# Bias table product among the unread transposes of the first norm, with 18 of them in place of 22

## The chip, the cores and the metric

The kernel runs on one core of a Trainium2 chip. What counts is the device time of one execution in microseconds (us): 847.76 us before, the median of 3 runs (847.65 to 847.85).

The core has five engines that run side by side and meet only at semaphores: PE (TensorE: matmuls and transposes; its weight loads are shown apart as PEld), DVE (VectorE), ACT (ScalarE), POOL (GpSimd) and SP (SyncE, which here only issues transfers). Each takes its own instructions in order. Transfers are issued from the queues of SP, ACT and POOL and are moved by 16 DMA engines that all of them share.

## What is computed

One decoder layer on a sequence of 512 tokens with 1024 channels. The first sub-layer normalises x, projects it once, and gives the columns to an attention mixer with 8 heads and to a recurrent mixer with 8 heads; both are projected back, merged by gates and added to x. The second is a gated feed-forward block. Of the reference, this matters here:

```python
h = rmsnorm(x, attn_norm_g[l])
proj = h @ w_in[l]
...
bias = bias_tab[t5_bucket(dist)]          # rel_bias: 32 buckets x 8 heads
sc = jnp.einsum('bqgrd,bkgd->bgrqk', q_b, kw) + bias
```

Each attention score gets a bias that depends on the head and on the bucket of the distance between query and key. The table `rel_bias` has 32 rows and 8 columns.

## The kernel before

**Dense products.** All weights are float32. A weight tile arrives in one of three buffers `raw` (512 KB, issued on SP's queue, line 265). ACT rounds it to a high part `whi` (line 123, the helper of all activations), DVE or POOL subtracts to get the low part `wlo` (line 294), and PE adds three products: high by high, high by low and low by high (line 120, the helper of all matmuls). A `raw` buffer is free for the next load when its low part has been made.

**The first norm.** Four tiles `xt` of 128 tokens are loaded on SP's queue (line 152). On ACT's queue go the identity matrix `ident`, a part of the tile `kc` (line 153), and the gains `pr0` (line 154). Eight small loads `pra` and the rest of `kc` go on POOL's. Three weight tiles are loaded behind `xt`. Then follows a stretch whose order of instructions is written out by hand. PE runs `NWARM` = 22 transposes of the identity into a bank that nobody reads (line 332); the gains' transpose (line 165) was put after 14 of them. ACT squares the four tiles and sums each (with a root for each pair); DVE makes the inverse roots and scales the tiles to `h` (line 130, one half tile on ACT). PE turns `h` by transposes (line 341: 8 for each of the first two tiles, then 8 pairs for the last two). ACT and DVE turn each result into the high part `hh` and the low part `hl`. With these, PE starts its first dense product. Eight PSUM banks are in use: four under the name `ps_mm`, two under `ps_a`, two under `ps_b`; the unread transposes write into one of `ps_b`, and the last two of the eight turned banks are `ps_b` too.

**The bias table.** The bias for each distance is a product: `oh`, a one-hot matrix of 33 rows and 384 distances, by `rbx`, the 32 rows of `rel_bias` and a row of -1e30 for forbidden distances. The result, 8 heads by 384, goes from PSUM to `vb` on ACT. One DMA then writes 16 copies of it into a DRAM tensor `vd`, from which eight transfers on SP's queue (line 902) read the shifted rows 80 us later. In the kernel before, all of this stands between the query projection and the projection of keys and values, in parts of the tile `QK` that the keys fill later. It isn't in an order written by hand; the scheduler put it there:

```python
pt = pa()
mm(pt[0:8, 0:384], rbx, oh, True, True)
act(vb, pt[0:8, 0:384])
```

While this runs, DVE inverts the triangular blocks of the recurrence (62 dependent operations, line 135, and then transposes, lines 728 and 733). PE uses their result in small correction products (`ps_a<-sg,AB`, 32 rows by 32), then starts the compression of keys and values (`ps_mm<-raw,sg`) and the recurrence over 8 chunks, with dense products filling its waits.

## Time and profile before

| What | us |
|---|---|
| median of the runs | 847.76 |
| the profiled execution, its time | 847.76 |
| the profiled execution, its span | 846.0 |
| PE busy | 831.9 |
| DVE busy | 514.7 |
| ACT busy | 405.7 |
| POOL busy | 52.5 |
| first unread transpose on PE | 4.89 |
| first dense matmul on PE | 14.16 |
| bias table product on PE | 152.73 |

A row of the timeline gives the start in us from the span's start, the length in us, the engine (a q behind its name: its queue issued a transfer), the line, the operation, the tile written and the tiles read, their shapes and how many instructions the row joins. Brackets give the engine's idle time just before and what ended it; "issue" stands for none that the profile shows. The ends of matmuls are modelled, and each row has a tail in which the next instruction already runs: the distance of two starts tells what an instruction costs PE. A row that joins several lasts until the end of the last.

### The profile page before, as it was taken

To read this page: it belongs to the slowest core of one execution; us is meant where nothing else is said; L and a number is where in the kernel's file an instruction comes from. 1 tells how busy PE (TensorE), PEld (TensorE's weight loads), DVE (VectorE), ACT (ScalarE), POOL (GpSimd) and SP (SyncE) were. 2 spreads that over 40 slices of the span, in tenths; PEclk is the share of its full clock that TensorE was granted. 3 is DMA by queue.
4 is the path that set the end of the run, shared out by engine and by line. 5 is a ranking of instruction groups with operands and counts; after the bars stand their busy time and mean duration, and the time that the engine had idled before them with its cause. 6 is when DMAs were issued, how large, how long until landed. Compare 5 with 4: busy or idle time off the path is not lost.

```text
span 846.0 us, 12844 instructions
## 1 busy us (share of the span) xinstructions
PE 831.9 (98%) x5097; PEld 676.2 (80%) x5097; DVE 514.7 (61%) x998; ACT 405.7 (48%) x784; POOL 52.5 (6%) x69
## 2 busy tenths in 40 slices
PE   7999999999999999999999999999999999999998
PEld 6777778897777886777788888888888888888886
DVE  5477779963555678888675566666666666322222
ACT  6766645443545677767344454444444444221210
POOL 6200020140000110111000000000000000000000
PEclk9999999999999999999999999999999999999999
DMA  7432222335551320010167023333333332333421
GB/s 231 112 86 62 75 75 76 92 108 151 132 119 50 83 69 13 15 36 26 52 215 221 0 77 98 100 100 100 100 100 95 90 91 98 100 100 112 136 75 50
DMA packets 109104, 78.73 MB, mean 93 GB/s; under 512 B 3869, under 2 KB 97748, under 8 KB 109044
## 3 DMA queue, kind: packets, MB, share of 16 engines
q1 hardware_dynamic: 106512, 73.51, 29.8%
q0 software_dynamic: 1472, 1.86, 1.0%
q10 hardware_dynamic: 1060, 2.55, 1.0%
q8 instruction: 40, 0.66, 0.3%
q14 instruction: 20, 0.16, 0.1%
HBM read 74.56 MB, written 2.29 MB: 91 GB/s over the span
## 4 chain that ended last, share of the span: by engine, by line
PE 52%; DVE 0%; ACT 0%; DVEq 0%; issue 0%
PE ps_mm L120 52%; DVE hl L135 0%; PE ps_a L120 0%; PE ps_b L1181 0%; PE ps_a L200 0%; PE ps_mm L1181 0%; ACT hh L123 0%; PE ps_b L200 0%; DVE x L126 0%; DVEq L1373 0%; PE ps_a L1133 0%
## 5 line engine op out<-in xcount | busy, mean ns | idle before, releaser
L294 DVE TENSOR_TENSOR wlo<-raw,whi 128x1024 fp32r<-128x1024 f32 (+1 forms) x111 | 131.6, 1185 | 189.4 <-PE ps_mm L120 166.8
L120 PE MATMUL ps_mm<-hh,whi 128*128 128x512 f32 (+1 forms) x624 | 243.3, 392 | 0.4 <-ACT hh L123 0.3
L120 PE MATMUL ps_mm<-hl,whi 128*128 128x512 f32 (+1 forms) x624 | 240.9, 388 | 0.3 <-DVE hl L135 0.2
L123 ACT ACTIVATE whi<-raw 128x1024 fp32r<-128x1024 f32 (+3 forms) x124 | 123.4, 996 | 170.3 <-PE ps_mm L120 142.4
L120 PE MATMUL ps_mm<-hh,wlo 128*128 128x512 f32 (+1 forms) x624 | 151.8, 385 | 0.0
L120 PEld LDWEIGHTS ps_mm<-hh,whi 128*128 128x128 f32 x624 | 117.3, 188 | 27.3 <-issue 1.3
L120 PEld LDWEIGHTS ps_mm<-hl,whi 128*128 128x128 f32 x624 | 117.4, 188 | 24.1 <-DVE hl L135 1.0
L120 PEld LDWEIGHTS ps_mm<-hh,wlo 128*128 128x128 f32 x624 | 115.2, 188 | 23.3
L120 PE MATMUL ps_mm<-whi,aT 128*128 128x512 f32 x352 | 84.5, 390 | 0.0
L120 PEld LDWEIGHTS ps_mm<-whi,aT 128*128 128x128 f32 x352 | 65.9, 188 | 14.3 <-issue 0.4
L135 DVE SCALAR_TENSOR_TENSOR cgv<-ps_mm,cw,cgv 128x511 f32<-128x511 f32 (+1 forms) x88 | 65.4, 746 | 1.5
L123 ACT ACTIVATE cgv<-ps_mm,cw 128x512 f32<-128x512 f32 x44 | 34.3, 781 | 22.8 <-PE ps_mm L120 22.8
L120 PE MATMUL ps_mm<-wlo,aT 128*128 128x512 f32 x176 | 44.3, 390 | 0.0
L123 ACT ACTIVATE P<-P,nm 128x512 f32<-128x512 f32 (+3 forms) x64 | 35.4, 554 | 14.9 <-DVE nm L1155 14.9
L123 ACT ACTIVATE aT<-cgv 128x512 fp32r<-128x512 f32 x22 | 13.9, 631 | 56.8 <-DVE cgv L126 56.8
L120 PEld LDWEIGHTS ps_mm<-wlo,aT 128*128 128x128 f32 x176 | 33.1, 188 | 6.9
L123 ACT ACTIVATE cgv<-cgv 128x512 f32<-128x512 f32 x22 | 13.9, 632 | 43.9 <-DVE cgv L135 43.8
L294 POOL TENSOR_TENSOR wlo<-raw,whi 128x512 fp32r<-128x512 f32 (+3 forms) x13 | 20.4, 1573 | 203.6 <-PE ps_mm L120 147.9
L1155 DVE CUSTOM_DVE_ANT_0 P<-ps_a,AB 128x512 f32<-128x512 f32 (+3 forms) x64 | 29.4, 484 | 4.2 <-PE ps_a L120 3.7
L126 DVE TENSOR_TENSOR x<-x,ps_mm 128x512 f32<-128x512 f32 (+1 forms) x17 | 11.1, 656 | 23.9 <-PE ps_mm L120 22.7
L126 DVE TENSOR_TENSOR aT<-cgv,aT 128x512 fp32r<-128x512 f32 x22 | 15.2, 693 | 14.7 <-ACT aT L123 14.7
L120 PE MATMUL ps_a<-KH,qst 128*128 128x512 f32 (+3 forms) x64 | 21.3, 349 | 1.5 <-DVE nm L1155 0.9
(356 smaller groups left out, 1205.5 us busy)
## 6 DMA issues: line engine op xcount, KB each, us to landing
raw<-in_w_up_dram SPq DMA_DIRECT2D x44, 512.0 KB, 3.8
raw<-in_w_in_dram SPq DMA_DIRECT2D x38, 512.0 KB, 3.9
raw<-in_w_down_dram SPq DMA_DIRECT2D x22, 512.0 KB, 3.6
raw<-in_w_out_dram SPq DMA_DIRECT2D x8, 512.0 KB, 3.7
xt<-in_x_dram SPq DMA_DIRECT2D x4, 512.0 KB, 5.7
raw<-in_cmp_w_k_dram SPq DMA_DIRECT2D x4, 512.0 KB, 4.0
raw<-in_cmp_w_v_dram SPq DMA_DIRECT2D x4, 512.0 KB, 4.4
raw<-in_w_proj_b_dram SPq DMA_DIRECT2D x8, 256.0 KB, 2.7
```

Source lines behind the costliest of these rows:

```text
L120: te.matmul(o, lhsT=l, rhs=r, start=start, stop=stop)
L123: sc.activation(o, i, f, **kw)
L126: v.tensor_tensor(o, a, b, op=op)
L135: v.scalar_tensor_tensor(o, a, s, b, op0=op0, op1=op1)
L294: eng.tensor_tensor(lo, raw, hi.bitcast(F32), op=ALU.subtract)
L1155: v.tensor_tensor_reduce(out=P[:, i], in0=sp[:, N * (i - i0):N * (i - i0) + N], in1=BT[:, h, 384 - 128 * qt:512], scale=-1.0, scalar=-NEG, ...
```

## The change

The bias table's product, its eviction and its store move to the first norm. `oh`, `rbx` and `vb` become tiles of their own. Their loads are issued on ACT's queue right behind the identity, ahead of the gains. The row of -1e30 is set by DVE instead of POOL. The product stands on PE behind the sixth unread transpose, into the second `ps_b` bank; `NWARM` falls from 22 to 18. The eviction stands on ACT between the squares of the third and the fourth tile. The store goes on SP's queue, behind the first three weight loads, instead of ACT's.

```diff
-    NWARM = 22
+    NWARM = 18
...
     sc.dma_start(ident, A["consts"][:, 0:128])
+    oh, rbx, vb = (xp.tile([p, n], F32, name=k) for k, p, n in (("oh", 33, 384), ("rbx", 33, 8), ("vb", 8, 384)))
+    v.memset(rbx[32:33], NEG)
+    sc.dma_start(rbx[0:32], A["rel_bias"])
+    sc.dma_start(oh, A["onehot"])
     sc.dma_start(pr0, A["attn_norm_g"][0].rearrange("(r p) -> r p", p=128))
...
+    vd = dp.tile([8, 16 * 385], F32, name="vd")
...
         warm = pb()
+        vps = pb()
         for i in range(NWARM):
             te.transpose(warm[:, 0:128], ident, ident)
+            if i == 5:
+                mm(vps[0:8, 0:384], rbx, oh, True, True)
...
         for t in (2, 3):
             act(hs[t], xt[:, t], AF.Square, accum_out=ssx[:, t:t + 1])
+            if t == 2:
+                act(vb, vps[0:8, 0:384])
+                nc.sync.dma_start(vd.rearrange("h (i m) -> h i m", m=385)[:, :, 0:384],
+                                  vb[:, None, :].to_broadcast([8, 16, 384]))
...
-    oh, rbx, vb = QK[0:33, 2048:2432], QK[0:33, 2440:2448], QK[0:8, 2560:2944]
-    nc.gpsimd.memset(rbx[32:33], NEG)
-    sc.dma_start(rbx[0:32], A["rel_bias"])
-    sc.dma_start(oh, A["onehot"])
-    pt = pa()
-    mm(pt[0:8, 0:384], rbx, oh, True, True)
-    act(vb, pt[0:8, 0:384])
-    vd = dp.tile([8, 16 * 385], F32, name="vd")
-    sc.dma_start(vd.rearrange("h (i m) -> h i m", m=385)[:, :, 0:384], vb[:, None, :].to_broadcast([8, 16, 384]))
```

In the order of instructions that the changed program ends up with, PE runs 6 unread transposes, the product, the gains' transpose and 12 unread transposes. Transfers share eight completion counters in turn, and three more early ones shift the turns: on SP, the first weight load now waits until the identity has landed, the second until the first tile of x, the third until the second. Before, only the third waited, for the identity. The last of the turned banks waits for the eviction, since it reuses the product's bank. On all engines the order of everything else is as before, but for ACT's evictions of keys and values next to the old place, which come tile by tile.

## The prediction

> **What bounds the kernel now.** I read the page's first lines, then the busy time by stretch (start and end, length, then PE, weight loads, DVE, ACT, POOL, the granted clock, the DMA engines' share and GB/s), then the timeline at the two places that the change touches.

> ```profile
> span 846.0 us, 12844 instructions
> PE 831.9 (98%) x5097; PEld 676.2 (80%) x5097; DVE 514.7 (61%) x998; ACT 405.7 (48%) x784; POOL 52.5 (6%) x69
> ...
> 4.88:14.16 9.28, 9.24 (x56) 8.22 (x56) 4.92 (x18) 8.13 (x15) 3.15 (x7) 1.00 1.10 342
> 14.16:150.00 135.84, 135.15 (x721) 104.13 (x722) 103.44 (x173) 84.03 (x176) 17.55 (x22) 1.00 0.31 81
> ...
> 156.00:168.00 12.00, 12.00 (x84) 11.16 (x84) 11.46 (x23) 4.83 (x25) 2.01 (x1) 1.00 0.30 71
> ```

> The profiled execution took 847.76 us, which is the median too: 846.0 of span and 1.76 around it. In 14.16 to 150 PE is busy 135.15 of 135.84, in 156 to 168 all of 12.00, so a microsecond taken from PE's order there, or added ahead of it, moves the end by as much, unless another engine is just behind. The 4.88 to 14.16 stretch is different: PE is as full, but with transposes whose output nobody reads. There the first norm sets the time. The question is what the product saves at 153 us and what it costs before 14 us.

> **What leaves, at 153 us.** The columns are start, length, engine, line, operation.

> ```profile
> 152.41 0.28 PE L120 MATMUL ps_mm<-spare,hl 128*128 128x256 f32 x1
> 152.53 0.28 PE L120 MATMUL ps_mm<-spare,hh 128*128 128x256 f32 x1
> ...
> 152.73 0.81 PE L120 MATMUL ps_a<-QK 33*8 33x384 f32 x2
> 153.06 0.48 PE L120 MATMUL ps_a<-QK 33*8 33x384 f32 x1
> ...
> 153.47 0.39 PE L120 MATMUL ps_mm<-spare,hl 128*128 128x256 f32 x1
> ...
> 153.58 0.48 ACT L123 ACTIVATE QK<-ps_a 8x384 f32<-8x384 f32 x1 [0.96 <-PE ps_a L120]
> ...
> 154.98 0.28 ACT L123 ACTIVATE QK<-ps_mm 128x128 f32<-128x128 f32 x1 [0.92 <-PE ps_mm L120]
> ```

> The projection's matmuls follow each other at 0.12 (152.41 to 152.53). Around the product, two instructions 0.33 apart, they are 0.94 apart (152.53 to 153.47). PE gains 0.94 - 0.12 = 0.82. The eviction (0.48) stands between two idle times of ACT, 0.96 and 0.92: it goes for nothing, as do the issues on ACT's queue and the one-row memset on POOL.

> Does another engine take the 0.82 back? The nearest is DVE, whose inversion and its transposes run unbroken beside PE.

> ```profile
> 163.02 4.51 DVE L728 STREAM_TRANSPOSE sg<-inv 32x1024 f32<-32x1024 f32 x2
> ...
> 168.72 0.10 PEld L120 LDWEIGHTS ps_a<-sg,AB 32*32 32x32 f32 x1 [0.35 <-issue]
> ...
> 180.30 1.29 DVE L126 TENSOR_TENSOR sg<-QK,prm 128x248 f32<-128x248 f32 x2
> ...
> L120 PE MATMUL ps_mm<-raw,sg x64: 378/380/430, 183.0 to 212.3; 128*64 128x256 f32 x64
> ```

> The correction products read sg, ready at 167.53, and start at 168.72: 1.19 of room. The compression's read at 183.0 has 1.4 after 181.59. Both exceed 0.82. Term one: **-0.82**.

> **What arrives, before 14 us.** PE's order becomes 6 transposes, the product, the gains' transpose (L165 now), 12 transposes: 18 for 22. Side by side, the two programs' orders show nothing else moved on PE.

> ```profile
> 4.89 3.25 PE L332 MATMUL ps_b<-kc 128*128 128x128 f32 x14 [4.89 <-DMA kc<-in_consts_dram]
> ...
> 8.07 0.27 PE L165 MATMUL ps_a<-kc,pr 8*128 8x8 f32 x1
> ...
> 8.27 1.97 PE L332 MATMUL ps_b<-kc 128*128 128x128 f32 x8
> ...
> 10.11 0.55 PEld L341 LDWEIGHTS ps_mm<-kc,h 128*128 128x128 f32 x4 [0.28 <-DVE h L130]
> 10.11 0.79 PE L341 MATMUL ps_mm<-kc,h 128*128 128x128 f32 x4
> ...
> 11.18 0.60 PE L341 MATMUL ps_mm<-kc,h 128*128 128x128 f32 x4
> 11.61 0.38 PE L341 MATMUL ps_a<-kc,h 128*128 128x128 f32 x2
> ...
> 12.12 1.13 PE L341 MATMUL ps_mm<-kc,h 128*128 128x128 f32 x8
> 12.63 2.42 ACT L123 ACTIVATE hh<-ps_mm,ang 128x512 fp32r<-128x512 f32 x4 [0.42 <-PE ps_mm L341]
> ...
> 15.47 0.19 PEld L120 LDWEIGHTS ps_mm<-hl,whi 128*128 128x128 f32 x1 [0.32 <-DVE hl L135]
> ```

> Of the unread transposes 14 take 3.25 and 8 take 1.97, so one takes (3.25 - 1.97)/6 = 0.21. Of the turns, of the same shape, four start between 11.18 and 11.61: 0.11 each. The four at 10.11 take 0.79, in between. So PE runs at half rate until about 10.4, though the granted clock stands at 1.00 all along. Four fewer save 0.85. The product's two parts at half rate are 2 x 2 x 0.33 = 1.32, plus 0.15 for the changes of weights (152.53 to 152.73 is 0.20 in place of 0.12, 153.06 to 153.47 is 0.08 over 0.33). The train grows by 1.32 + 0.15 - 0.85 = 0.6. It ended at 10.0 (8.27 + 8 x 0.21) and ends near 10.6, or 10.5, as its last few run at the faster rate. The first turn could start at 10.11, when DVE had its tile; now PE makes it wait. Sixteen turns at 0.11 take 1.8 and end near 12.3, so the pair at 12.12, which releases hh at 12.63, starts 0.2 later. From there the delay goes through hh and hl to PE, which waits for hl at 15.47.

> [...]

> **When the operands land** decides more. PE must have them by 6.2 (4.89 + 6 x 0.21).

> ```profile
> 0.75 0.40 ACTq L153 DMA_DIRECT2D kc<-in_consts_dram  x1
> ...
> 1.26 0.54 ACTq L154 DMA_DIRECT2D pr<-in_attn_norm_g_dram  x1
> ...
> 4.70 1.06 ACT L123 ACTIVATE h<-xt 128x1024 f32<-128x1024 f32 x1 [2.01 <-DMA xt<-in_x_dram]
> ...
> 6.00 1.06 ACT L123 ACTIVATE h<-xt 128x1024 f32<-128x1024 f32 x1 [0.15 <-DMA xt<-in_x_dram]
> ...
> 5.00:6.00 1.00, 1.00 (x5) 1.00 (x6) 0.00 (x0) 0.85 (x2) 0.46 (x1) 1.00 1.03 409
> ...
> pra<-in_rwkv_w_dram POOLq DMA_DIRECT2D x1, 2.0 KB, 5.4
> ...
> QK<-in_onehot_dram ACTq DMA_DIRECT2D x1, 49.5 KB
> ...
> QK<-in_rel_bias_dram ACTq DMA_DIRECT2D x1, 1.0 KB, 1.4
> ```

> The two new loads take pr's place in ACT's queue, at about 1.3 and 1.8; pr goes third. In a quiet stretch such a load lands after 1.4, which gives 3.2. Under the x loads, which fill the engines (409 GB/s), the identity needed 4.1 (0.75 to 4.89) and a 2 KB load on POOL's queue 5.4. So the one-hot table lands between 3.2 and 7.2. I take the identity's 4.1 (5.9) plus 0.3 to 0.7 for third place, 6.2 to 6.6: it is nearest in queue and size. A wait of 0.3 replaces unread transposes that would run at half rate by ones after the rise, and costs 0.1. So the start costs 0.3. The gains' transpose behind the product needs pr, one place later, at about 7.9: 1.3 more than the table.

> **Beside it, at nothing.** ACT's eviction of the product stands between the squares.

> ```profile
> 8.34 0.19 ACT L123 ACTIVATION_READ_ACCUMULATOR h<-xt 128x1 f32 x1
> 8.91 1.06 ACT L123 ACTIVATE h<-xt 128x1024 f32<-128x1024 f32 x1 [0.38 <-DMA xt<-in_x_dram]
> ...
> 10.52 1.06 ACT L123 ACTIVATE whi<-raw 128x1024 fp32r<-128x1024 f32 x1
> 11.48 0.73 ACT L123 ACTIVATE h<-xt,ssx 128x512 f32<-128x512 f32 x1
> ...
> 2.64 2.27 SPq L265 DMA_DIRECT2D raw<-in_w_in_dram  x2
> ...
> 15.59 0.37 SPq L265 DMA_DIRECT2D raw<-in_w_in_dram  x1
> ```

> Its 0.48 fills ACT's 0.38 of waiting for the fourth x tile, so the fourth square is 0.1 late, inside PE's 0.2; without that cover it would be 0.48, and behind it wait the second root, the first weight's rounding at 10.52 and the half tile at 11.48. If the product ended after 8.5, ACT and these would wait with it. On SP, the order of the changed program makes the first weight load wait for the identity (4.89) instead of going at 2.64. The x loads ahead hold the engines to 8.91, so it is still queued 3 us early; were it not, up to 2.25 would fall on 10.52. The 49.5 KB of table at 409 GB/s push everything behind it back 0.12, again beside PE's delay. The table's store, now on SP behind the third weight load, has only the load at 15.59 after it, held by POOL: nothing. The memset goes to DVE, idle then.

> **Sum.** -0.82 + 0.2 + 0.1 = -0.5: 847.76 - 0.5 = **847.2**. Bounds of this case: start cost 0 (clock up early) to 0.6 (operands at 7.0), so 846.9 to 847.5.

> **Rivals.**
> *The table is late.* If each small load lets one quarter of x (1.30, 4.70 to 6.00) go ahead, the identity follows the first, rel_bias the second, the table the third, which lands about 7.3. The product runs 7.5 to 8.9, the gains follow, and twelve transposes end near 11.2 with the rate rising at 10.4; turns end at 13.0, a start cost of 0.9 (ACT's fourth square, 0.5 late behind the eviction, lies beside it). Net +0.1: **847.8**, no gain. For it: POOL's 5.4. Against: the identity's 4.1. [...] No row here settles it, as pr's landing is hidden.

> *The clock rises late* (the slower side). The product uses 33 rows and 8 columns, perhaps after an idle gap; if this doesn't keep the rate's rise at 10.4 and all 16 turns run at 0.21, they end at 10.6 + 3.4 = 14.0 instead of 12.1, start cost 1.9, net +1.1: **848.9**. It decides from an operand landing past about 7, or if so small a product doesn't count. For it: the rate rose at 10.4 after 5.5 us of full-width work without a gap, and no row shows that less would do. Against it: 18 of the 22 transposes stay. [...]

> *The gain is absorbed* at 168.72: if DVE ran 0.7 late against PE there, 0.3 of the 0.82 would go and the sum would be **847.5**. DVE's whole chain starts from PE's own results, so it moves with it.

> **Chances.** Forecast 0.52, table late 0.26, clock late 0.15, absorbed 0.04, other 0.03. The range 846.7 to 848.6 holds the forecast's own 846.9 to 847.5, the late table, the absorbed gain and the lighter part of the clock's case; its ends lie 0.2 past the forecast's lower bound and 0.3 short of that case's price. About 0.2% (1.7 us) is what a measurement of this kernel tells from no change: below 846.1 would need twice the product's price, 0.03; above 849.5 takes the clock's case with a longer wait, 0.08; between, 0.89.

> **What would show it.** After: no product near 153 us and 0.12 between the projection's matmuls; the product on PE at 6.3 to 6.7 without a long wait for its loads; first hh 0.2 to 0.4 after 12.63; the product at 168.72 about half a microsecond earlier. A start of the product past 7, or turns 0.21 apart after 10.6, shows a rival; a first rounding that waits for its weight past 10.7 shows that the load's wait on SP wasn't hidden.

## The result and the profile after

The changed kernel takes 851.64 us, the median of 6 runs (850.79 to 851.98), against 847.86 for the kernel before on the same chip (847.65 to 848.04): a ratio of 1.0044, 95% interval 1.0031 to 1.0056. It is slower by 3.8 us, where the forecast was 0.5 faster; the time lies 3.0 above the top of the range. The profiled execution took 851.36, with a span of 849.6.

Three stretches show where. First the start, PE's timeline (start, length, engine, line, operation):

```profile
5.10 1.54 PE L340 MATMUL ps_b<-kc 128*128 128x128 f32 x6 [5.10 <-DMA kc<-in_consts_dram]
6.62 1.43 PE L120 MATMUL ps_b<-oh,rbx 33*8 33x384 f32 x2
7.98 0.27 PE L169 MATMUL ps_a<-kc,pr 8*128 8x8 f32 x1
8.19 2.82 PE L340 MATMUL ps_b<-kc 128*128 128x128 f32 x12
10.80 1.06 PE L355 MATMUL ps_mm<-kc,h 128*128 128x128 f32 x4
...
12.34 0.60 PE L355 MATMUL ps_mm<-kc,h 128*128 128x128 f32 x4
...
15.16 0.50 PE L120 MATMUL ps_mm<-hh,whi 128*128 128x512 f32 x1
```

The product stands at 6.62, where the forecast had it, and its row shows no wait for the table. But the four turns at 10.80 still take 0.21 each; only those at 12.34 are at 0.11. PE's rate rises at about 12.1 instead of 10.4, and the first dense matmul starts at 15.16 instead of 14.16: +1.0. Of this the longer train is about 0.6, as forecast, and the six turns at half rate about 0.4. Another 0.2 is chance: the identity landed at 5.10 instead of 4.89, and three kernels without the early table had it at 4.99 to 5.20. Small waits of PE that fell away give back 0.2.

The product is gone at 153, and the gain is there: PE reaches the correction products at 168.78 instead of 168.72, so 0.94 of the 1.0 is back. There it is lost again. DVE and POOL of the kernel before, then of the changed one:

```profile
162.57 0.19 DVE L135 SCALAR_TENSOR_TENSOR Tm<-inv 128x31 f32<-128x31 f32 x1
162.79 0.19 DVE L135 SCALAR_TENSOR_TENSOR inv<-Tm,inv 128x31 f32<-128x31 f32 x1
...
163.09 2.01 POOL L294 TENSOR_TENSOR wlo<-raw,whi 128x840 fp32r<-128x840 f32 x1 [13.98 <-PE ps_mm L120]
```

```profile
163.03 0.22 DVE L135 SCALAR_TENSOR_TENSOR Tm<-inv 128x60 f32<-128x60 f32 x1
163.29 1.91 DVE L135 SCALAR_TENSOR_TENSOR inv<-Tm,inv 128x60 f32<-128x60 f32 x1
...
165.68 4.34 DVE L732 STREAM_TRANSPOSE sg<-inv 32x1024 f32<-32x1024 f32 x2
...
163.04 2.08 POOL L298 TENSOR_TENSOR wlo<-raw,whi 128x840 fp32r<-128x840 f32 x1 [35.22 <-PE ps_mm L120]
...
168.78 0.24 PE L120 MATMUL ps_a<-sg,AB 32*32 32x32 f32 x2
170.07 0.21 PE L120 MATMUL ps_b<-sg,AB 32*32 32x32 f32 x1 [1.05 <-DVE sg L732]
```

Before, DVE's inversion ends at 162.98 and POOL's subtract starts 0.11 behind it. After, POOL is where it was, since PE releases it and PE has made up the late start; DVE's chain began at 124, ahead of the removed product, and is 1.0 late. So POOL's 2.08 falls on the inversion, and a step of 0.22 lasts 1.91, about until POOL is done (165.12; the step ends at 165.20). Its row has no bracket, so the view shows no wait ahead of the step but a longer step: here the engines don't meet at semaphores alone. sg is ready at 170.02 instead of 167.53, and PE waits.

Busy time by stretch (columns as in the prediction), before and then after:

```profile
168.00:172.00 4.00, 4.00 (x141) 3.57 (x139) 3.94 (x3) 3.04 (x6) 1.97 (x1) 1.00 0.16 41
172.00:176.00 4.00, 4.00 (x87) 3.80 (x86) 3.95 (x7) 1.80 (x3) 0.00 (x0) 1.00 0.42 134
```

```profile
168.00:172.00 4.00, 2.94 (x127) 2.43 (x127) 3.94 (x3) 1.95 (x4) 1.96 (x1) 1.00 0.09 31
172.00:176.00 4.00, 4.00 (x34) 3.96 (x28) 3.96 (x3) 1.63 (x3) 0.00 (x0) 0.57 0.49 135
```

Behind the wait the granted clock is 0.57 in the mean of these 4 us; it stands at 0.50 from 172.57 to 175.98. (The counts, 34 and 87 matmuls, aren't of the same ones: before, many 32x32 products fall into this stretch.) The 280-wide matmuls, which start at 172.21 (170.87 before), follow each other at 0.23 until 176.0: 17 of them take 3.83 instead of 2.30, so 1.5 more.

Last, the weight loads of the recurrence, three in a set. SP's first issue and ACT's rounding of the last tile, for the second and the third set, after:

```profile
195.83 0.37 SPq L269 DMA_DIRECT2D raw<-in_cmp_w_k_dram  x1
...
205.72 0.37 SPq L269 DMA_DIRECT2D raw<-in_cmp_w_k_dram  x1
...
203.37 1.06 ACT L123 ACTIVATE whi<-raw 128x1024 fp32r<-128x1024 f32 x1 [7.08 <-DMA raw<-in_w_in_dram]
214.10 1.06 ACT L123 ACTIVATE whi<-raw 128x1024 fp32r<-128x1024 f32 x1 [3.58 <-DMA raw<-in_w_in_dram]
```

From the first issue to the rounding the second set takes 7.54 and the third 8.38; before it was 7.26 (192.95 to 200.21) and 7.70 (202.55 to 210.25). That is 0.3 and 0.7 more, of which the loads behind them give back 0.2. With that the profiled execution adds up: start +1.0, product -0.94, wait +1.28, clock +1.5, loads +0.8, together 3.6.

### The profile page after: what moved, and what is told of

Same layout as the page of the kernel before. It is cut to its first block, busy times and chain, and to the rows that moved or that the text cites. A ratio compares the mean times of both kernels' runs of the same rounds, so it can differ in the third digit from the quotient of the medians.

```text
span 849.6 us, 12834 instructions
## 1 busy us (share of the span) xinstructions
PE 833.4 (98%) x5093; PEld 677.2 (80%) x5093; DVE 516.3 (61%) x999; ACT 407.0 (48%) x784; POOL 52.3 (6%) x68
## 4 chain that ended last, share of the span: by engine, by line
PE 52%; DVE 0%; ACT 0%; DVEq 0%; issue 0%
PE ps_mm L120 51%; DVE hl L135 0%; PE ps_a L120 0%; PE ps_b L1185 0%; PE ps_a L204 0%; PE ps_mm L1185 0%; ACT hh L123 0%; PE ps_b L204 0%; DVE x L126 0%; DVEq L1377 0%; PE ps_a L1137 0%
## 5 line engine op out<-in xcount | busy, mean ns | idle before, releaser
L120 PE MATMUL ps_mm<-hh,whi 128*128 128x512 f32 (+1 forms) x624 | 242.9, 391 | 0.4 <-ACT hh L123 0.3
L120 PE MATMUL ps_mm<-hl,whi 128*128 128x512 f32 (+1 forms) x624 | 240.6, 387 | 0.3 <-DVE hl L135 0.2
L123 ACT ACTIVATE whi<-raw 128x1024 fp32r<-128x1024 f32 (+3 forms) x124 | 123.3, 995 | 170.9 <-PE ps_mm L120 142.3
L120 PE MATMUL ps_mm<-hh,wlo 128*128 128x512 f32 (+1 forms) x624 | 151.8, 384 | 0.0
L120 PEld LDWEIGHTS ps_mm<-hh,whi 128*128 128x128 f32 x624 | 117.2, 188 | 27.5 <-issue 1.0
L120 PEld LDWEIGHTS ps_mm<-hl,whi 128*128 128x128 f32 x624 | 117.3, 188 | 24.1 <-DVE hl L135 1.0
L120 PEld LDWEIGHTS ps_mm<-hh,wlo 128*128 128x128 f32 x624 | 115.1, 188 | 23.4
L120 PE MATMUL ps_mm<-whi,aT 128*128 128x512 f32 x352 | 84.5, 390 | 0.0
L120 PEld LDWEIGHTS ps_mm<-whi,aT 128*128 128x128 f32 x352 | 65.9, 188 | 14.3 <-issue 0.4
L135 DVE SCALAR_TENSOR_TENSOR cgv<-ps_mm,cw,cgv 128x511 f32<-128x511 f32 (+1 forms) x88 | 65.4, 746 | 1.5
L123 ACT ACTIVATE cgv<-ps_mm,cw 128x512 f32<-128x512 f32 x44 | 34.4, 781 | 23.1 <-PE ps_mm L120 23.1
L120 PE MATMUL ps_mm<-wlo,aT 128*128 128x512 f32 x176 | 44.3, 389 | 0.0
L123 ACT ACTIVATE P<-P,nm 128x512 f32<-128x512 f32 (+3 forms) x64 | 35.4, 553 | 14.9 <-DVE nm L1159 14.9
L123 ACT ACTIVATE aT<-cgv 128x512 fp32r<-128x512 f32 x22 | 13.9, 631 | 56.8 <-DVE cgv L126 56.8
L120 PEld LDWEIGHTS ps_mm<-wlo,aT 128*128 128x128 f32 x176 | 33.0, 188 | 6.9
L123 ACT ACTIVATE cgv<-cgv 128x512 f32<-128x512 f32 x22 | 13.9, 632 | 43.2 <-DVE cgv L135 43.2
L126 DVE TENSOR_TENSOR x<-x,ps_mm 128x512 f32<-128x512 f32 (+1 forms) x17 | 11.0, 655 | 23.5 <-PE ps_mm L120 22.0
L126 DVE TENSOR_TENSOR aT<-cgv,aT 128x512 fp32r<-128x512 f32 x22 | 15.2, 692 | 14.7 <-ACT aT L123 14.7
L120 PE MATMUL ps_mm<-whi,hh 128*128 128x280 f32 (+2 forms) x72 | 23.8, 347 | 0.2 <-DVE AB L126 0.2
```

The costliest lines, as they stand in the source:

```text
L120: te.matmul(o, lhsT=l, rhs=r, start=start, stop=stop)
L123: sc.activation(o, i, f, **kw)
L126: v.tensor_tensor(o, a, b, op=op)
L135: v.scalar_tensor_tensor(o, a, s, b, op0=op0, op1=op1)
```

## The experiments

The theory after this reading: without the product at 153, POOL's subtract falls on DVE's inversion (**collision**); the start adds its own. Rivals: the start's delay alone upsets the later order, or the early transfers do. In all kernels the order on the engines is that of the kernel they are made from, but for the edit; in e16 and e17 the rounding of one weight tile on ACT and a few instructions on DVE around its subtract have moved too. Each result gives the median, in brackets the lowest and the highest execution, then the ratio to the kernel before, measured beside it, with its 95% interval.

**e1, both products.** The changed kernel with the old product back at its place:

```diff
+    oh2, rbx2, vb2 = QK[0:33, 2048:2432], QK[0:33, 2440:2448], QK[0:8, 2560:2944]
...
+    mm(pt[0:8, 0:384], rbx2, oh2, True, True)
+    act(vb2, pt[0:8, 0:384])
```

> The changed kernel, with the old product (its two loads, matmul and eviction, no store) kept at the old place as well; the result of the second one is not used. Theory (collision): leaving 0.82 us out of PE's order at 153 lets POOL's subtract of the first key/value-gate tile (128x840, 2.0 us) start before DVE's inversion has ended; one DVE step then takes 1.9 in place of 0.22, sg comes late, PE waits about 1 us and then runs at a lower clock. With the 0.82 back on PE, POOL starts about 0.1 after the inversion's end as before, so only the start's 1.0 is left: 848.8 (848.4 to 849.2), no DVE step over 0.5 us between 160 and 166, correction products start without a wait. Rival 1 (the start's delay alone shifts everything into the bad order): 851.6 or more, 852.4. Rival 2 (the three early transfers and shifted completion turns are the cause): 852.4.

850.72 (849.80 to 851.94), ratio 1.0033 (1.0020 to 1.0045). The place was right and the sum wrong by 1.9. The collision is gone: POOL starts at 164.85, behind the inversion's end at 164.69, PE doesn't wait, the clock stays at 1.00. But in this execution the start cost 1.8 (first dense matmul at 15.96; PE also waited 0.28 for the table), and the weight loads 7.85 and 8.21. The loads had been no part of the theory; from here they were.

**e2, no product at all**, from the kernel before:

```diff
-    mm(pt[0:8, 0:384], rbx, oh, True, True)
-    act(vb, pt[0:8, 0:384])
+    act(vb, oh[0:8])
```

> The kernel before, with the product left out altogether (vb is copied from the one-hot table, so the biases are not the reference's); loads, eviction and store stay at the old place, the start is untouched. Theory (collision): the removal at 153 is enough. POOL's subtract starts near 162.3, DVE's inversion step stalls until it ends, PE waits over 1 us at the correction products and the clock falls: 850.6 (849.5 to 851.3), slower than before although PE has less to do. Rival 1 (start's delay): 846.9, that is before less 0.82. Rival 2 (early transfers): 846.9.

850.65 (849.96 to 852.64), ratio 1.0035 (1.0022 to 1.0048): less work, start and transfers untouched (it leaves the product out and takes a copy of the one-hot table for `vb`), and slower by 2.7. DVE, POOL, and busy time by stretch:

```profile
162.35 1.98 DVE L135 SCALAR_TENSOR_TENSOR inv<-Tm,inv 128x60 f32<-128x60 f32 x1
...
162.24 2.01 POOL L294 TENSOR_TENSOR wlo<-raw,whi 128x840 fp32r<-128x840 f32 x1 [13.05 <-PE ps_mm L120]
```

```profile
168.00:170.00 2.00, 0.91 (x52) 0.80 (x52) 1.97 (x2) 1.21 (x2) 1.92 (x1) 1.00 0.00 0
170.00:172.00 2.00, 2.00 (x89) 1.94 (x83) 1.97 (x2) 1.24 (x3) 0.05 (x1) 0.62 0.22 29
```

POOL comes 0.85 earlier, DVE doesn't move, a step stalls, PE is busy 0.91 of 2.00 and the clock falls, to 0.50 from 170.47 to 177.30. The removal alone makes the collision. Both rivals had 846.9. The change also puts ACT's evictions of keys and values in another order; they aren't the cause, since e2 has the old order and collides, and e1 has the new one and doesn't. Not all of e2's loss comes from the collision: its third set of loads takes 8.31 (see e7).

**e3, a late start alone**: the kernel before with `NWARM = 33`.

> The kernel before with 33 unread transposes in place of 22: a start delay alone, product at its old place. Theory (collision): PE, DVE and POOL all move by the same, so the delay adds up once: first dense matmul about 1.0 later (15.1), time 848.7 (848.4 to 849.2). Rival 1 (the start's delay upsets the order later): 851.4. Rival 2 (early transfers): 848.7.

847.95 (847.42 to 849.61), ratio 1.0003 (0.9994 to 1.0012), where the theory had 848.7. In the profiled execution the first dense matmul moved by only 0.4 (14.58): the rate rose at 8.75 already, ahead of the place where its train outlasts that of the kernel before, so all turns were at 0.11. PE had made the 0.4 up by 226. It speaks against the first rival, but tests it with 0.4, not with 1.0.

**e4, a gate**: in the changed kernel POOL first copies an element of the finished inverse.

```diff
+            if gate and n == 280:
+                eng.tensor_copy(lo[:, 0, 0:1], gate.pop())
             eng.tensor_tensor(lo, raw, hi.bitcast(F32), op=ALU.subtract)
```

> The changed kernel, with POOL made to wait: ahead of the subtract of the first key/value-gate tile it copies one element of the finished inverse, so that it can't start while DVE's inversion runs. All other orders are the same. Theory (collision): no DVE step stalls, sg is ready near 168.6, PE waits 0.2 at most, the clock stays: 848.0 (847.5 to 848.5), 3.5 faster than the changed kernel. Rival 1 and rival 2: 851.6, as the stall is not the cause; or the wait only moves (POOL later, PE waits for wlo): 850 to 852.

849.22 (848.84 to 851.10), ratio 1.0018 (1.0008 to 1.0027): 2.4 less than the changed kernel.

```profile
164.46 0.18 POOL L299 CAST wlo<-inv 128x1 fp32r<-128x1 f32 x1 [36.26 <-DVE inv L135]
164.72 2.01 POOL L300 TENSOR_TENSOR wlo<-raw,whi 128x840 fp32r<-128x840 f32 x1
```

```profile
172.00:176.00 4.00, 4.00 (x87) 3.80 (x86) 3.96 (x3) 1.80 (x4) 0.00 (x0) 1.00 0.45 131
```

POOL on the gate, then busy time by stretch: no stall, no wait, and the clock at 1.00. That it isn't 848.0 has two causes in the profiled execution: a start of +1.4 (15.55) and weight loads of 7.85 and 8.37.

**e5, the gate in the kernel before** (the same edit, where nothing collides).

> Control: the kernel before with POOL's one-element copy of the finished inverse ahead of the subtract of the first key/value-gate tile. In the kernel before this subtract starts 0.1 after the inversion's end anyway. Theory (collision of POOL's subtract with DVE's inversion): nothing to win, POOL starts 0.3 later, 847.9 (847.6 to 848.2). Rival (the wait on DVE helps or harms for itself, whatever the collision): a change of over 0.5 either way.

847.95 (847.33 to 848.69), ratio 0.9999 (0.9990 to 1.0007): no effect of the gate itself shows.

**e6, the product at full width**, from the changed kernel:

```diff
-    ... (("oh", 33, 384), ("rbx", 33, 8), ("vb", 8, 384)))
+    ... (("oh", 128, 384), ("rbx", 128, 128), ("vb", 8, 384)))
+    nc.gpsimd.memset(oh, 0.0)
+    v.memset(rbx, 0.0)
...
-                mm(vps[0:8, 0:384], rbx, oh, True, True)
+                mm(vps[:, 0:384], rbx, oh, True, True)
```

> The changed kernel with the product's operands padded by zeros to 128 rows and 128 columns (same 384 columns of output, same time on PE). Theory (a product of 33 rows by 8 columns doesn't count for the rise of PE's rate): the rate rises near 10.4 to 10.8 instead of 12.0 to 13.2, first dense matmul at 14.5 to 14.8 instead of 15.2 to 16.0; the rest as in the changed kernel, 850.6 to 851.2. Rival (what breaks the run is the wait of 0.3 for the table ahead of the product, whatever its size): rise at 12.0 to 13.2 as before, 851.6.

849.82 (849.36 to 851.92), ratio 1.0028 (1.0018 to 1.0038): 1.8 less.

```profile
6.57 1.62 PE L120 MATMUL ps_b<-oh,rbx 128*128 128x384 f32 x2
...
8.32 2.09 PE L342 MATMUL ps_b<-kc 128*128 128x128 f32 x12
10.24 0.62 PE L357 MATMUL ps_mm<-kc,h 128*128 128x128 f32 x4
...
14.65 0.50 PE L120 MATMUL ps_mm<-hh,whi 128*128 128x512 f32 x1
```

The same 384 columns in the same place, but the twelve transposes take 2.09 instead of 2.82 and all turns are at 0.11: the rate rises at 9.5. So the product's 33 rows by 8 columns had held up the rise, not a wait. The 1.8 isn't the start's alone, as the clock behind the wait has a part in it: six of e6's nine executions had a mean clock of 0.999 or 1.000 (849.36 to 850.80) and three 0.997 or 0.998 (851.24 to 851.92), while five of the changed kernel's six had the lower one. Against those five, the three are 0.6 shorter in the median. The collision is still there (a DVE step of 2.01), though in this execution the clock stayed at 1.00 behind a wait of 1.23.

**e7, eight tiny matmuls** (1x1) ahead of the unread transposes, in the gated kernel, while PE waits for the identity:

```diff
+        for i in range(8):
+            mm(warm[0:1, 0:1], one, one, True, True)
```

> The gated kernel of e4 with 8 matmuls of 1x1 ahead of the unread transposes, while PE waits for the identity; so PE has 4 instructions more than in the kernel before in place of 4 fewer. Theory (the late loss of 1.2 between 193 and 216 is partly a fetch of instructions, 16 KB on one DMA engine for 1.0 us, which comes 3.3 us after the first of three weight loads instead of ahead of their data, since PE's place in its code has moved): the fetch falls near 202.5 again, the third set of loads is 0.7 shorter, 848.5 (848.2 to 848.8). Rival (the transfers' counters or the SP queue's waits slow the loads): 849.2 as in e4.

848.11 (847.41 to 849.55), ratio 1.0002 (0.9993 to 1.0011): 1.1 less than e4 for matmuls that do nothing, with the same late start (15.61). The DMA queues while the third set's data move: e4 (204.70 to 212.02), then e7 (204.80 to 211.12; packets, MB, share of 16 engines):

```profile
q1 hardware_dynamic: 2096, 1.57, 73.6%
q8 instruction: 1, 0.02, 0.9%
```

```profile
q1 hardware_dynamic: 2091, 1.57, 83.2%
```

In e4 one packet of q8, the queue that the view calls instruction, falls among the data (0.9% of 16 engines in 7.32 us is 1.05 us on one of them); in e7, with eight matmuls more on PE, none does, and the set takes 7.38 instead of 8.37. The same view has such a packet among the third set's data in the changed kernel, e1 and e2 too, where the set takes 8.38, 8.21 and 8.31, and no packet of q8 in e9 and the kernel before, where it takes 7.33 and 7.70. e6 and e14 take 8.56 and 8.49 and all others 7.1 to 7.6; where the packet falls in these, no view shows. The six with 8.2 to 8.6 are also the only ones whose PE has fewer instructions than the kernel before: 5093 or 5095 for 5097.

**e9, all three repairs**: gate, tiny matmuls, full-width product.

> All three repairs on the changed kernel: POOL's gate (e4), the 8 tiny matmuls ahead (e7) and the product padded to 128 by 128 (e6). Theory (three separate costs that add): start 0.9 to 1.0 earlier than e7 (first dense matmul at 14.6), POOL behind the inversion, instruction fetch ahead of the third loads: 847.2 (846.9 to 847.6), 0.8 less than before. Rival (the costs overlap, one hides behind another): 847.9 to 848.2.

848.12 (847.25 to 849.37), ratio 1.0002 (0.9993 to 1.0010). The profiled execution is the fastest, 847.25, with the first dense matmul at 14.59; the median is 0.9 above it. The repairs didn't add up in the median, which is where the rival (847.9 to 848.2: one cost hides behind another) had it; why the other executions are longer, no trace shows.

**e8 and e10, an early train**: in the gated kernel matmuls of a zero tile from 1.1 us on, 26 unread transposes, the gains' transpose by hand. With 18 of them (e8, 847.88, ratio 0.9996, 0.9987 to 1.0004) they lasted to 7.7, and the first dense matmul came at 15.42 instead of the expected 14.0 to 14.3; with ten:

```diff
+        for i in range(10):
+            mm(warm[:, 0:128], wz, wz, True, True)
```

> e8 with 10 matmuls of a zero tile in place of 18 (in e8 they took 0.37 each and lasted until 7.7; ten end near 4.8, when the identity lands). Theory (PE's rate up before the product, nothing late): product at 6.5 to 6.9 in 0.8, turns from 10.1 at 0.11, first dense matmul at 14.0 to 14.3, 846.7 (846.3 to 847.3). Rival (the wait for the table ahead of the product, or the product, brings the rate down again): turns at 0.21, first dense matmul at 15 or later, 847.7 to 848.2.

847.05 (846.55 to 848.40), ratio 0.9992 (0.9983 to 1.0000). The product takes 0.80 and all turns are at 0.11. The profiled execution is the longest of the eleven (848.40), so its start is not that of the median: in it ACT waits for the first weight tile, and the first dense matmul comes at 15.46.

```profile
11.85 1.06 ACT L123 ACTIVATE whi<-raw 128x1024 fp32r<-128x1024 f32 x1 [0.85 <-DMA raw<-in_w_in_dram]
```

**e11, the same early train in the kernel before.**

> Control: the kernel before with the same 10 early matmuls and 34 unread transposes, product at its old place. Theory (before, the first norm's data and not PE's rate set the start): first dense matmul at 14.0 to 14.2, 847.8 (847.5 to 848.0). Rival (the early matmuls are a gain by themselves, and e10 owes its gain to them): 847.0 or less.

847.56 (847.38 to 847.84), ratio 0.9998 (0.9989 to 1.0006): the train gains little by itself.

**e12 and e14, the store on ACT's queue**, the one line undone in e7 and in the changed kernel:

```diff
-                nc.sync.dma_start(vd.rearrange(...
+                sc.dma_start(vd.rearrange(...
```

> e7 with the table's store issued on ACT's queue in place of SP's, so that SP has as many transfers as in the kernel before. Open: the second set of three weight loads (193 to 201) takes 7.5 to 7.9 from the first issue to the rounding in every kernel with the early table, and 7.2 to 7.3 in the others. Theory (one transfer more on SP's queue shifts something of its order): 7.3 again, 847.6 (847.3 to 847.9). Rival (it has another cause): 7.7 and 848.1 as in e7.

> The changed kernel with one line undone: the table's store on ACT's queue instead of SP's, at its new place. Theory: collision, start and clock stay, the second set of weight loads takes 7.2 to 7.3 instead of 7.5 to 7.9: 851.2 (850.6 to 851.5). Rival (the store's queue is of no account while PE is late anyway): 851.6.

e12: 847.98 (847.45 to 849.49), ratio 1.0002 (0.9993 to 1.0011); e14: 850.82 (850.04 to 852.86), ratio 1.0040 (1.0027 to 1.0054). In both the second set is quick again. e12's issues and rounding:

```profile
193.06 0.37 SPq L269 DMA_DIRECT2D raw<-in_cmp_w_k_dram  x1
...
200.26 1.06 ACT L123 ACTIVATE whi<-raw 128x1024 fp32r<-128x1024 f32 x1 [6.73 <-DMA raw<-in_w_in_dram]
```

That is 7.20 for e7's 7.74, and 7.24 in e14. Over all kernels the second set takes 7.2 to 7.4 with the store on ACT's queue and 7.5 to 8.0 with it on SP's. How one transfer more on SP does this 180 us later, no run shows. The medians don't show the gain. On ACT the store's issue, ahead of the fourth square, holds up that square by 0.87. e12's median is 0.1 below e7's; e14's five executions fall into three at a mean clock of 1.000 (850.04 to 850.82) and two at 0.996 (852.65 and 852.86), and its median decides nothing. e14's late start (first dense matmul at 16.15) isn't the store's: PE runs without a gap from the first turn at 10.93 to the pairs at 14.21, with 14 of the 16 turns at 0.21.

**e13, e10 with that store.**

> e10 (gate, ten early matmuls, gains' transpose by hand) with the table's store on ACT's queue as in e12. Theory (the named costs are all there is): e10's 847.05 less the 0.5 that the second set of weight loads gains: 846.6 (846.2 to 847.2), faster than the kernel before by more than 0.8. Rival (something else is left): 847.0 or more, as e10.

847.67 (847.26 to 848.20), ratio 0.9997 (0.9988 to 1.0006): worse than e10. ACT's timeline:

```profile
9.63 0.79 ACTq L356 DMA_DIRECT2D vd<-vb  x1
10.47 1.06 ACT L123 ACTIVATE h<-xt 128x1024 f32<-128x1024 f32 x1 [0.87 <-ACT vb L123]
```

The fourth square waits 0.87 for the issue, and the pairs of turns start at 13.31.

**e15, PE kept busy**: the changed kernel with six unread 128x512 matmuls ahead of the correction products.

```diff
+        busy = pb()
+        for i in range(6):
+            mm(busy, hh[:, i, 0:128], hh[:, i], True, True)
         below(0)
```

> The changed kernel with 6 matmuls of 128x512 into a bank that nobody reads, put on PE ahead of the first correction products, where PE waits for sg (1.4 of work for a wait of 1.05 to 1.3). Theory (the wait makes the granted clock fall at 172 to 176, worth about 1.1 to 1.4): clock 1.00 throughout, 280-wide matmuls at 0.13, 850.5 (850.1 to 851.0). Rival (the clock falls for another reason, such as the small products themselves, or its fall costs nothing at the end): 851.6 to 852.

849.89 (849.05 to 850.47), ratio 1.0022 (1.0013 to 1.0031): 1.45 us of useless work, and 1.75 less time (0.6 less than expected).

```profile
172.00:176.00 4.00, 4.00 (x73) 3.80 (x68) 3.94 (x3) 2.00 (x4) 0.00 (x0) 1.00 0.48 134
```

DVE's step still takes 1.91, but the clock stays at 1.00. Not all of the 1.75 is the clock's: the third set takes 7.44, for 8.38 in the changed kernel. Of the changed kernel's own runs five had a mean clock of 0.997 or 0.998 and 851.3 to 852.0, one had 1.000 and 850.79; that puts the clock at about 1, with whatever else sets these executions apart.

**e16, the store behind the norm**: e10 with the store issued on ACT after its last `hh`.

> e10 with the table's store issued on ACT's queue behind the first norm's last evictions (in e13 its issue stood ahead of the fourth square and held that up by 0.87). Theory: second set of weight loads 7.2 to 7.3 as in e12, the squares as in e10: 846.6 (846.2 to 847.0). Rival (the issue on ACT holds up the second or third weight's rounding and then PE): 847.0 or more.

846.92 (846.49 to 847.53), ratio 0.9987 (0.9979 to 0.9996): it beats the kernel before beyond its interval, by 1.1 us. From e10 it can't be told apart. First dense matmul at 14.35, no wait at 168, sets of loads in 7.4 and 7.6. **e17** takes the table's loads to POOL's queue as well:

> e16 with the two table loads on POOL's queue ahead of the eight small ones, so that the first two weight loads wait for nothing, as in the kernel before. Theory (the wait for the identity, 4.9 in place of 2.7, makes the first weight late for ACT's rounding when PE is early): no wait of ACT for raw at 10.5 to 11.9, first dense matmul at 14.0 to 14.3, 846.4 (846.0 to 846.9). Rival (POOL's queue lands the table later than ACT's, past 7.5, and PE waits): product at 7.5 or later, 847.0 or more.

847.15 (846.77 to 849.01), ratio 0.9996 (0.9987 to 1.0005). The first weight tile is only 0.16 late, but the table lands later: PE waits 0.77 for `rbx`, the product starts at 7.78. No gain. Three of its eleven executions had a mean clock of 0.998 and took 848.52 to 849.01; no trace shows where the clock fell in them.

## Why the prediction was wrong, point by point

**The product's 0.82 at 153: right.** PE got it (0.94 by 168.7).

**"Both exceed 0.82": the step that failed.** The room of 1.19 at 168.72 was worked out as if DVE's chain had a fixed length. The sentence on the rival, "DVE's whole chain starts from PE's own results, so it moves with it", holds for a late start but not for work removed at 153, behind the chain's start at 124. And POOL's subtract, which PE releases, did move against the chain: it had 0.11 of room, not 1.19. The trace of before shows both rows; the prediction quoted the row of the transposes at 163.02 and never set POOL's row beside it. It also shows the price: at 177.32 a DVE step that takes 0.16 elsewhere (176.64) takes 1.34 beside a POOL subtract of 1.41.

```profile
176.64 0.16 DVE L126 TENSOR_TENSOR rs_y<-kss 128x8 f32<-128x8 f32 x1
...
177.22 1.41 POOL L294 TENSOR_TENSOR wlo<-raw,whi 128x560 fp32r<-128x560 f32 x1 [6.33 <-ACT AB L123]
177.32 1.34 DVE L126 TENSOR_TENSOR rs_y<-kss 128x8 f32<-128x8 f32 x1
```

Why POOL's subtract makes a DVE step longer, no trace shows. The traces show how long: 1.91 to 2.01 in place of 0.22 in five kernels (the changed kernel, e2, e6, e14 and e15), beside a POOL subtract of 2.00 to 2.08, while before, the one-input transposes at 163.02 ran through POOL's 2.01 at nearly their usual length (4.51 for two; 4.34 in the changed kernel). e2 shows it made by the removal alone, e4 and e5 that it costs 2.4 with what follows from it.

**"The gain is absorbed" (0.04, 847.5)** named the place, with 0.3 lost. The wait was 1.05 to 1.23, and behind it came what no rival had: the clock at 0.50 for 3.4 us, in e2 for 6.8.

**The start, 0.3: mis-sized; it cost 0.9 to 2.0** in the profiled executions with this start (first dense matmul at 15.06 to 16.15). The train grew as forecast; what failed is the rise, taken to stay at 10.4 (12.14 in the changed kernel). The rival "the clock rises late" was right in its condition, "if so small a product doesn't count" (e6). Its price of 1.9, with all 16 turns at 0.21, is the upper end: in the changed kernel six were, in e14 fourteen.

In the seven profiled executions with the narrow product among the unread transposes at half rate (the changed kernel, e1, e4, e7, e12, e14, e15) the rise came at 11.86 to 14.06, in the six with the old warm-up or the wide product (the kernel before, e2, e3, e5, e6, e9) at 8.75 to 10.80. What sets its place within these ranges, no run shows; the changed kernel's 12.14 is near the early end. The 1.00 that the prediction read beside the half rate is not a granted clock: the record of the kernel before begins with the rise, at 10.43, and time without a record counts as 1.00 in the row.

That the operands would be in time was right in the changed kernel (no wait for `oh`), though e1, e4, e12 and e14 waited 0.22 to 0.42. "The table is late" did not come, and that each small load lets one quarter of x go ahead, from which that rival's 7.3 is worked out, no run shows: the product started at 6.62 in the changed kernel, at 6.68 to 7.11 in those four.

**"Beside it, at nothing": half wrong.** The eviction of `vb` was covered. The store on SP was not: 0.3 to 0.6 in the second set of loads. The first weight load's wait for the identity left the sign that the prediction named (the first rounding at 11.05, behind a wait of 0.28), and was covered as long as PE was late itself. With PE early it was 0.85 of ACT's time in e10's profiled execution, 0.16 in e17's and nothing in e16's.

**Not seen at all:** the third set of loads, 0.7 to 1.0 longer with a q8 packet among its data, which eight matmuls more on PE took out of them (e7).

**What remains of the change.** With the collision gated, the rate up early and the store out of the way, the early product gains 1.1 (e16). The same early train without it gains 0.3 (e11). The difference is about the product's 0.82, but each of the two is known only to some 0.7, so that the whole 0.82 arrives is likely, not shown.

## What to carry to other kernels

Work taken from one engine moves everything that this engine releases against everything that began earlier: before counting a gain, look at which pair of engines then runs at the same time (here a DVE step of 0.22 took 1.91 beside a POOL subtract). A slack is the smallest room of any neighbour at the place (here 0.11), not the room of the one wait that comes to mind. Early work that is put among warm-up matmuls can cost the warm-up: here a product of 33 rows by 8 columns had the rate rise at 12.1, the same padded to 128 by 128 at 9.5.
